# A hybrid attention and recurrence block: both value projections as one block product of seven, attention weights by differences of the values, and gate inputs kept in DRAM

## The chip, the cores and the metric

The kernel runs on one core of a Trainium2 chip. The core has a matrix engine (TensorE, PE in the profile), three engines for elementwise work (VectorE or DVE, ScalarE or ACT, GpSimd or POOL), a fifth engine that only issues transfers (SyncE or SP), and 16 DMA engines that move data between DRAM and the two on-chip memories, SBUF (operands, 128 partitions) and PSUM (results of matmuls, 8 banks of 512 columns of fp32). The metric is the device time of one execution in microseconds, lower is better; a kernel's time is the median of several executions.

## The reference

One layer on x (1024 tokens x 1024 channels, fp32), followed by a final RMSNorm:

```python
xn = rmsnorm(x, norm1_g);  u = xn @ w_in           # 3*512 + 4*512 + 2*1024 columns
q_sb, k_sb, v_sb, f_raw, i_hg, q_hg, g_hg, gate_sb, gate_hg = split(u)
# stick-breaking attention, 8 heads of 64; for query t and key s < t:
A[t, s] = sigmoid(z_ts) * prod_{s<j<t} (1 - sigmoid(z_tj)),   z = q.k / 8
o_sb = A @ v_sb
# gated recurrence (HGRN2), 4 heads of 128: S_t = diag(f_t) S_{t-1} + (1 - f_t) i_t^T, o_t = S_t^T q_t
o_hg = rmsnorm(hgrn2(silu(q_hg), f, i_hg)) * silu(g_hg)
merged = sigmoid(gate_sb + b) * (o_sb @ w_o_sb) + sigmoid(gate_hg + b) * (o_hg @ w_o_hg)
h = x + merged @ w_out
h = h + square(relu(rmsnorm(h, norm2_g) @ w_ff1)) @ w_ff2
return rmsnorm(h, final_g)
```

v_sb (512 columns) and i_hg (512 columns) are the values of the attention and of the recurrence; both are plain projections of xn.

## The kernel before, in words

Operands of matmuls are split in two: a high part, rounded by a cast (ScalarE, `hi_copy`, line 144), and a low part, the remainder (VectorE, `lo_sub`, line 149). A product is then three matmuls, high x high, high x low and low x high (`three`, line 526). One helper issues all matmuls (line 121), another all transposes (line 124), another SP's loads (line 129), so in the profile they share a line and are told apart by their tiles: pjqk, pjf, pjq, pjg are projections, pjv and pji the two value projections, z the attention's scores, pw the transposed weights, po its output, pga and pgq parts of the gate projections, gX and gY the gate products.

The program is written straight out, with no loop on the chip. A scheduler assigns each engine its instructions in order, from the order in which they are written, their data and a few hand-made order edges (`after`). TensorE's work is written in two lanes: "main" (attention, recurrence) and "fill" (projections that nobody waits for at once). Fill work is cut into steps of a few matmuls and dealt out between the pieces of the main lane: a stream `st` holds a list of jobs (one job: split its weights, then the steps of its matmuls, then an epilogue), `st.advance(n, upto)` issues n steps, `st.finish(upto)` the rest of the jobs up to a number. While one job runs, the next job's weights are split and those of the one after are loaded (`prefetch`); the first job has nobody ahead of it to do so. `turns` holds the order of ScalarE's and VectorE's instructions during the first norms as written.

The stages, with rough times in the profile:

- 0 to 50 us: x is loaded, normalised, transposed and split into `xn` (high and low, by token half and pairs of k-tiles). Beside that, head 0's q and k, and the values of heads 0 to 3 ("quad 0", `first_job`, `token_steps`): per block of 128 tokens 8 k-tiles x 3 matmuls of 256 columns. The first block runs its matmuls on the weights' high parts first (`lo_last`).
- 50 to 315 us: the attention, 64 items (8 heads x 8 query blocks, in the order 7, 0, 6, 1, 5, 2, 4, 3). For an item `scores` makes z and two sigmoids from it, bt = sigmoid(z) and rm = sigmoid(-z); `weights` runs a product scan over rm from the right on VectorE (line 777) and multiplies bt by it (line 157); `turn` transposes bt on TensorE and splits it into high and low; `values` multiplies by V. In between come 126 fill steps: q and k of heads 1 to 7, the values' quad 1, the recurrence's f, q, first values (`i_job`, 256 columns wide again) and g of head 0.
- 302 to 580 us: the recurrence, head by head (`hg_levels`, then `hg_tail` beside the next head's levels), with fill steps at the rates `FILL`: the other recurrence projections, `raw_job` (eight, each a block of the gate projections that needs no sums) and `sb_job` (the attention's output projection).
- 500 to 600 us: `whole_input` adds xn's high and low parts back together by DMA, and `sum_forms` makes sums and differences of its four blocks and splits them: forms 6, 5, 7 and 3, for the gate projections, which are already a 2x2 by 2x2 block product of seven (`GatePair`: x6, y5, x7, y3).
- 580 us to the end: gates, output projection and the MLP.

Of the kernel before, what the change touches and what calls it, by code (L numbers as in the profile page):

```python
# [39 lines left out]
def kernel(  # L40
# [37 lines left out]
    def slot_n(name, n, dt=F32):  # L78

        if n <= 512:  # L80
            return hpool.tile([P, 512], dt, tag="h", name=name)
        return slot(name, dt)

# [440 lines left out]
    st = Stream()  # L524
# [109 lines left out]
    vt, qk, osb = {}, {}, {}  # L634

    def v_epilogue(quad):


        def ep(ps, tb):
            if tb % 2 == 0:  # L640
                vt[quad, tb // 2] = slot(f"V{quad}_{tb // 2}", F32R)
            V = vt[quad, tb // 2].rearrange("p (t h s d) -> p t h s d", t=2, h=4, s=2)
            src = ps.rearrange("p (h d) -> p h d", h=4)
            hi_lo(V[:, tb % 2, :, 0, :], V[:, tb % 2, :, 1, :], src)

        return ep

    def v_stat(h, tb):
        c = ((tb % 2) * 4 + h % 4) * P
        return vt[h // 4, tb // 2][:, c : c + P]  # L650
# [15 lines left out]

    def v_unit(quad):
        return wide_unit(f"wv{quad}", W_IN, C_V + quad * 256)

    def v_job(quad):  # L670
        unit = v_unit(quad)
        return st.add(
            [unit], lambda: token_steps(f"pjv{quad}", unit, xn, range(NT), v_epilogue(quad))
        )
# [27 lines left out]

    def first_job():
        name, u_qk, ep = qk_item(0)
        u_qk.__class__ = FirstUnit
        u_v = v_unit(0)

        def body():
            v_ep = v_epilogue(0)
            for half, parts in enumerate((((0, 2), (2, 2)), ((0, 4),))):  # L710
                ps = bank(f"{name}_{half}")
                for b0, n in parts:
                    ts = slice(b0 * P, (b0 + n) * P)
                    yield from proj_half(ps[:, ts], u_qk.hl[0], xn.mov, KT, half, ts=ts)
                    if b0 + n == 4:
                        ep(ps, half)
                    if half == 0 and b0 > 0:
                        st.prefetch()
                    tb = 4 * half + b0
                    yield from token_steps("pjv0", u_v, xn, range(tb, tb + n), v_ep, tb == 0)  # L720

        return st.add([u_qk], body), u_qk, u_v

    j_first, u_qk0, u_v0 = first_job()
    j_qk = {0: j_first}
    for h in range(1, NHS):
        j_qk[h] = proj_jobs([qk_item(h)], xn)
        if h == 4:
            v_job(1)
# [6 lines left out]
    def scores(h, qb):  # L736
# [3 lines left out]
        bt, rm = slot_n(f"bt{h}_{qb}", nk), slot_n(f"rm{h}_{qb}", nk)  # L740
        step = 320 if nk == 640 else 512
        for s0 in range(0, nk, step):
# [3 lines left out]
            for i, Q in enumerate((QH, QL)):  # L746
# [7 lines left out]
            c0, e = int(s0 == 0), m - (s0 + m == nk)  # L754
            nc.scalar.activation(  # L755
                rm[:, s0 + c0 - 1 : s0 + m - 1], z[:, c0:m], AF.Sigmoid, scale=-0.125
            )
            nc.scalar.activation(bt[:, s0 : s0 + e], z[:, :e], AF.Sigmoid, scale=0.125)  # L758
        lastsel[0] = nc.gpsimd.memset(bt[:, nk - 1 : nk], 0.0)
        zs[h, qb] = (bt, rm)  # L760
# [4 lines left out]
    nc.vector.tensor_copy(bits[:, 1024 - P - 1 : 1023], ident)  # L765

    def weights(h, qb):
# [4 lines left out]
        bt, rm = zs[h, qb]  # L772
        cut = qb == NT - 1
        parts = ((512, nk - 1), (0, 512)) if cut else ((0, nk - 1),)
        for i, (a, b) in enumerate(parts):
# [11 lines left out]
            m = mul(bt[:, a:b], bt[:, a:b], rm[:, a:b])  # L787
            if qb == 5:
                after(m, turn_lo[0])

    def turn(h, qb, between):

        open_block("main")
        bt, rm = zs.pop((h, qb))
# [14 lines left out]
        if par == 0:  # L809
            for t in tiles[-1]:  # L810
                after(nc.gpsimd.memset(t[:, (nkb - 1) % 4, qs].bitcast(F32), 0.0), lastsel[0])
        order = list(enumerate(tiles))
        for i, (th, tl) in order[::-1] if qb == NT - 1 else order:
# [10 lines left out]
            turn_lo[0] = hi_lo(  # L824
                th[:, 0:n, qs], tl[:, 0:n, qs], pw[:, : n * P].rearrange("p (k q) -> p k q", q=P)
# [60 lines left out]
    def i_job(h):  # L886
        unit = wide_unit(f"wi{h}", W_IN, C_I + h * P)

        def ep(ps, tb):
            for j in range(2):  # L890
                if tb == 0:
                    hg[h + j, "v"] = slot(f"v{h + j}")
                nc.scalar.copy(hg[h + j, "v"][:, tb * P : (tb + 1) * P], ps[:, j * P : (j + 1) * P])

        unit.late = h == 0

        def body():
            for i, _ in enumerate(token_steps(f"pji{h}", unit, xn, range(NT), ep)):
                yield
                if unit.late and i == 6:  # L900
                    hi_behind[0] = turn_hi[0]
                    st.prefetch()
                    hi_behind[0] = None

        return st.add([unit], body)
# [10 lines left out]

    def hg_jobs(h):
        for key, c0, ep in (
            ("f", C_F, f_epilogue(h)),
            ("q", C_QH, silu_epilogue(h, "q")),  # L920
            ("g", C_GH, silu_epilogue(h, "g")),
        ):
            if key == "g" and h % 2 == 0:
                i_job(h)
            u = cols_unit(f"w{key}{h}", [(W_IN, c0 + h * P, P)])
            j_hg[h] = proj_jobs([(f"pj{key}{h}", u, ep)], xn)

    hg_jobs(0)
# [224 lines left out]
    class Split:  # L1153
# [18 lines left out]
    scratch = ctx.enter_context(  # L1172
        tc.tile_pool(name="scratch", bufs=1, space=bass.MemoryType.DRAM)
    )

    def dram(name, shape):
        return scratch.tile(shape, F32, tag=name, name=name)

    def half(name, dt=F32):
        return hpool.tile([P, 512], dt, tag="h", name=name)  # L1180

# [74 lines left out]
    def raw_job(cb):  # L1256
# [13 lines left out]
        def body():  # L1270
# [13 lines left out]
            if cb == 3 or cb == KT - 1:  # L1284
                whole_input(1, int(cb == KT - 1))
# [15 lines left out]
    forms, whole = {}, {}  # L1301
    WAIT = 5

    def whole_input(i, j):
        for kp in range(2):
            h, l = (t.bitcast(F32) for t in xn.t[i, 2 * j + kp])
            nc.gpsimd.dma_start(l, h, accum_op=ALU.add)
            whole[i, j, kp] = l

    def sum_forms():  # L1310


        raw = whole
        def split(m, kp, src):
            forms[m, kp] = tuple(slot(f"gs{n}{m}{kp}", F32R) for n in "hl")
            hi_lo(*forms[m, kp], src)

        for j in range(2):
            whole_input(0, j)
        yield from range(WAIT)  # L1320
        s1, s2 = {}, {}
        for kp in range(2):
            s1[kp], s2[kp] = slot(f"gs1{kp}"), slot(f"gs2{kp}")
            ins = add(s1[kp], raw[1, 0, kp], raw[1, 1, kp])
            if kp == 0:
                after(ins, hg_sum[0])
            yield
            sub(s2[kp], s1[kp], raw[0, 0, kp])
            yield
            split(6, kp, s2[kp])  # L1330
            yield
        for kp in range(2):
# [785 lines left out]
    for tb in range(3, NT):  # L2118
        load_x(tb)
# [181 lines left out]
```

## Time and profile before

| | |
|---|---|
| time, median of 3 runs | 1449.7 us (1448.64 to 1451.11) |
| the profiled execution's own time | 1450.06 us |
| its span, first to last instruction | 1448.3 us |
| busy: TensorE, VectorE, ScalarE, GpSimd | 1433.5, 1101.4, 668.4, 146.7 us |
| moved by DMA | 225.73 MB, mean 156 GB/s |
| granted TensorE clock | 0.999 |

How to read it: a profile's times count from the first instruction. A group of instructions is given by line, engine, operation and tiles (out<-in); then their number, busy time and mean duration, the engine's idle time just before them, and what ended it. Matmuls overlap in the record, each lasting longer than the time until the next begins, so for TensorE the time from start to start counts, not the duration. A window gives for each engine its busy time and, in brackets, its number of instructions, in the order PE, PEld (weight loads), DVE, ACT, POOL, as far as they have any; then the granted clock, the DMA engines' share and GB/s.

### The profile page before, as it was taken

What the parts mean: (1) busy time and instruction counts of PE and PEld (TensorE: products, weight loads), DVE (VectorE), ACT (ScalarE), POOL (GpSimd) and SP (SyncE); (2) the same over time, 40 slices, a digit from 0 to 9 for tenths busy, and PEclk for the clock granted to TensorE, in tenths of its full rate; (3) what the DMA queues carried; (4) which work ended last, traced back from release to release, by engine and by line L of the source; (5) the groups of instructions that cost most, each with busy time, mean ns of one, the idle gap of its engine ahead of it and who ended that gap; (6) DMA issues with size and microseconds to landing.
All of it is one profiled execution on the core that took longest, in us unless ns stands there. A gap on an engine that the chain in (4) does not pass through costs nothing. (4 is left out here: it accounts for less than half of the span.)

```text
span 1448.3 us, 19992 instructions
## 1 busy us (share of the span) xinstructions
PE 1433.5 (99%) x7470; PEld 1220.8 (84%) x7470; DVE 1101.4 (76%) x1571; ACT 668.4 (46%) x1156; POOL 146.7 (10%) x344
## 2 busy tenths in 40 slices
PE   9999999999999999999999999999999999999997
PEld 8989988988898888888887888888888888888886
DVE  6699899798747797887776898666666757768765
ACT  7566666652323243523243675444444533523343
POOL 3121121110000012100010300000000000000042
PEclk9999999999999999999999999999999999999999
DMA  7234154321303349655469514344445974776724
GB/s 212 48 99 102 37 95 81 60 44 52 103 16 102 73 138 258 233 166 177 146 188 312 192 59 164 134 153 160 151 155 193 344 275 175 256 271 251 277 101 180
DMA packets 157913, 225.73 MB, mean 156 GB/s; under 512 B 25676, under 2 KB 93816, under 8 KB 157816
## 3 DMA queue, kind: packets, MB, share of 16 engines
q1 hardware_dynamic: 141976, 181.19, 37.3%
q0 software_dynamic: 12096, 36.71, 10.3%
q10 hardware_dynamic: 3744, 6.56, 1.2%
q8 instruction: 59, 0.97, 0.3%
q14 instruction: 38, 0.31, 0.1%
HBM read 162.55 MB, written 61.87 MB: 155 GB/s over the span
## 5 line engine op out<-in xcount | busy, mean ns | idle before, releaser
L144 ACT CAST whid<-w 128x1024 fp32r<-128x1024 f32 x30 | 31.6, 1053 | 153.4 <-PE pm L121 85.5
L777 DVE TENSOR_TENSOR_SCAN rm<-rm,bits 128x511 f32<-128x511 f32 (+7 forms) x72 | 87.3, 1220 | 14.2 <-ACT rm L755 12.7
L121 PE MATMUL pm<-wlod,sh 128*128 128x512 f32 x240 | 93.5, 389 | 0.0
L121 PE MATMUL pm<-whid,sh 128*128 128x512 f32 x240 | 93.4, 389 | 0.0
L121 PE MATMUL pm<-whid,sl 128*128 128x512 f32 x240 | 93.4, 389 | 0.0
L121 PE MATMUL pm<-tl,sh 128*128 128x512 f32 (+1 forms) x210 | 81.3, 387 | 0.0
L121 PE MATMUL pm<-th,sl 128*128 128x512 f32 (+1 forms) x210 | 81.3, 387 | 0.0
L121 PE MATMUL pm<-th,sh 128*128 128x512 f32 (+1 forms) x210 | 81.3, 387 | 0.0
L149 DVE TENSOR_TENSOR wlod<-w,whid 128x1024 fp32r<-128x1024 f32 x30 | 36.7, 1224 | 56.0 <-ACT whid L144 56.0
L149 DVE TENSOR_TENSOR sl<-sa,sh 128x1024 fp32r<-128x1024 f32 x56 | 68.3, 1220 | 0.5 <-ACT sh L144 0.5
L144 ACT CAST wTh<-pw 128x128 fp32r<-128x128 f32 (+3 forms) x96 | 44.4, 487 | 50.2 <-PE pw L124 42.6
L1950 POOL TENSOR_SCALAR fss<-fss 128x1 f32<-128x1 f32 x8 | 4.4, 547 | 562.4 <-ACT fsc L1945 561.9
L144 ACT CAST sh<-sa 128x1024 fp32r<-128x1024 f32 x56 | 57.2, 1046 | 7.3 <-DMA sa<-ad 7.3
L149 DVE TENSOR_TENSOR wTl<-pw,wTh 128x512 fp32r<-128x512 f32 (+3 forms) x96 | 50.7, 547 | 8.8 <-ACT wTh L144 6.3
L121 PEld LDWEIGHTS pm<-wlod,sh 128*128 128x128 f32 x240 | 45.0, 188 | 9.8 <-DVE wlod L149 0.4
L121 PEld LDWEIGHTS pm<-whid,sl 128*128 128x128 f32 x240 | 45.1, 188 | 9.4
L121 PEld LDWEIGHTS pm<-whid,sh 128*128 128x128 f32 x240 | 45.1, 188 | 9.2
L157 DVE TENSOR_TENSOR bt<-bt,rm 128x511 f32<-128x511 f32 (+7 forms) x72 | 49.0, 686 | 4.9 <-ACT bt L758 1.0
L121 PE MATMUL pX<-sql,t1h 128*128 128x512 f32 x128 | 50.0, 391 | 0.4 <-DVE sql L149 0.4
L121 PE MATMUL pX<-sqh,t1h 128*128 128x512 f32 x128 | 50.0, 390 | 0.0
L121 PE MATMUL pX<-sqh,t1l 128*128 128x512 f32 x128 | 49.8, 389 | 0.0
L755 ACT ACTIVATE rm<-z 128x511 f32<-128x511 f32 (+6 forms) x96 | 47.5, 501 | 4.6 <-DVE bt L157 1.9
(924 smaller groups left out, 4598.7 us busy)
## 6 DMA issues: line engine op xcount, KB each, us to landing
w<-in_w_ff_dram SPq DMA_DIRECT2D x72, 512.0 KB, 5.9
sa<-ad SPq DMA_DIRECT2D x56, 512.0 KB, 6.9
ad<-a SPq DMA_DIRECT2D x32, 256.0 KB, 4.2
ad<-s SPq DMA_DIRECT2D x16, 512.0 KB, 5.5
tw<-in_w_out_dram POOLq DMA_DIRECT2D x24, 256.0 KB, 4.1
x<-in_x_dram SPq DMA_DIRECT2D x8, 512.0 KB, 8.7
xnl<-xnh POOLq DMA_DIRECT2D x8, 512.0 KB, 10.8
pr<-pd SPq DMA_DIRECT2D x8, 512.0 KB, 6.5
```

The source lines that it names most:

```text
L121: return pe(nc.tensor.matmul(*a, **k))
L144: hi_last[0] = after(in_turn("act", nc.scalar.copy(dst, src)), hi_behind[0])
L149: nc.vector.tensor_tensor(out=dst, in0=src, in1=hi.bitcast(F32), op=ALU.subtract),
L157: return nc.vector.tensor_tensor(out=out, in0=a, in1=b, op=ALU.mult)
L755: nc.scalar.activation(rm[:, s0 + c0 - 1 : s0 + m - 1], z[:, c0:m], AF.Sigmoid, scale=-0.125)
L777: sc = nc.vector.tensor_tensor_scan(out=rr, data0=rr, data1=bits[:, 1024 - nk + a : 1024 - nk + b][:, ::-1], initial=rm[:, b : b + 1] if i ...
L1950: nc.gpsimd.tensor_scalar(out=ssq, in0=ssq, scalar1=1.0 / D, scalar2=EPS, op0=ALU.mult, op1=ALU.add)
```

## The change

The two value projections become one product: xn as 2x2 blocks (token halves by halves of the 1024 channels) times the weights as 2x2 blocks (channel halves by attention's and recurrence's 512 columns), with seven block products in place of eight. Each is 4 token blocks x 4 k-tiles x 3 matmuls of 512 columns. It stands ahead of the attention; products 1 and 2, on plain blocks of the first token half, stand among the first norms in place of quad 0. Products 3, 5, 6 and 7 need sums and differences of xn's blocks: xn is added together on VectorE (`early_whole`), summed (`early_op`), split (`early_form`), and the split forms are stored to DRAM, where the gates read them back later instead of making them (`whole_input` and the old `sum_forms` go). The results are stored to DRAM by rows (`vrows`, `irows`) and loaded back by head.

The attention's weights are taken apart: with R_s the product of rm from s on, the weight is R_{s+1} - R_s, so that A @ v is the sum over s of (R_s - 1)(v_{s-1} - v_s). bt, its sigmoid and its product go; the scan runs over nk instead of nk - 1 columns; rm is transposed; 1 is subtracted as it is split (a bias on ScalarE, a scalar on VectorE); the values of a head are loaded twice, one row apart, subtracted and split (`v_load`, `v_split`).

The order of the fill jobs changes: head 1's q and k are finished ahead of the products (it is now the first job of `st`), raw jobs 0 and 1 move into the attention, g of recurrence head 0 out of it; 86 fill steps are left there. `FILL` is changed, and x6 and y5 of the first gate pair move into the last recurrence tail.

The diff, cut to its core:

```diff
+    class ValuePair:
+        WEIGHT = {1: "11", 2: "21", 3: "22", 4: "21", 5: "11", 6: "22", 7: "12"}
+        def sums(self):
+            for kp in range(2):
+                b11, b12, b21, b22 = (self.raw[b, kp] for b in ("11", "12", "21", "22"))
+                sub_(b11, b12, b11)
+                sub_(b12, b22, b12)
+                sub_(b22, b22, b11)
+                sub_(b21, b21, b22)
+        def steps(self, m, banks, start):
+            for k in range(4):
+                wh, wl = (t[:, (k % 2) * 512 : (k % 2 + 1) * 512] for t in self.hl[m, k // 2])
+                for tb, ps in banks.items():
+                    three(ps, *self.stat(m, k, tb), wh, wl, start and k == 0, k == 3, True)
...
+        def x7(self):
+            self.product(7, self.X, False)
+            for tb in range(4):
+                self.u3[tb] = half(f"vu3{tb}")
+                nc.scalar.copy(self.u3[tb], self.X[tb])
+                v = self.p4[tb]
+                nc.vector.tensor_tensor(out=v, in0=v, in1=self.X[tb], op=ALU.add)
+                self.store(vrows, 1, 1, tb, v)
...
+    def early_form(m, *src):
+        for kp, r in enumerate(src):
+            vi.form[m, kp] = tuple(slot(f"ef{n}{m}{kp}", F32R) for n in "hl")
+            hi_lo(*vi.form[m, kp], r)
+            for i, t in enumerate(vi.form[m, kp]):
+                nc.gpsimd.dma_start(formd[m, kp][:, i, :], t.bitcast(F32))
...
     def scores(h, qb):
-            nc.scalar.activation(
-                rm[:, s0 + c0 - 1 : s0 + m - 1], z[:, c0:m], AF.Sigmoid, scale=-0.125
-            )
-            nc.scalar.activation(bt[:, s0 : s0 + e], z[:, :e], AF.Sigmoid, scale=0.125)
-        lastsel[0] = nc.gpsimd.memset(bt[:, nk - 1 : nk], 0.0)
+            nc.scalar.activation(rm[:, s0 : s0 + m], z[:, :m], AF.Sigmoid, scale=-0.125)
     def weights(h, qb):
-            m = mul(bt[:, a:b], bt[:, a:b], rm[:, a:b])
     def turn(h, qb, between):
-                transpose(pw[:, kb * P : (kb + 1) * P], bt[:, s0 : s0 + P])
-            turn_lo[0] = hi_lo(th[:, 0:n, qs], tl[:, 0:n, qs], pw...)
+                transpose(pw[:, kb * P : (kb + 1) * P], rm[:, s0 : s0 + P])
+                    nc.scalar.activation(th[:, 0:n, qs], src, AF.Identity, bias=minus_one),
+                nc.vector.scalar_tensor_tensor(
+                    out=tl[:, 0:n, qs], in0=src, scalar=-1.0,
+                    in1=th[:, 0:n, qs].bitcast(F32), op0=ALU.add, op1=ALU.subtract,
...
     def sum_forms():
+        yield from range(7)
+        for i, m in enumerate((6, 5, 7, 3)):
+            for kp in range(2):
+                forms[m, kp] = tuple(slot(f"gs{n}{m}{kp}", F32R) for n in "hl")
+                for j, t in enumerate(forms[m, kp]):
+                    load(t.bitcast(F32), formd[m, kp][:, j, :])
+                yield
...
-    u_v0.roomy = (1,)
-    u_v0.load(1)
+    vi.load("11", 0)
     load_x(2)
-    u_v0.load()
-    for tb in range(3, NT):
+    vi.load("11", 1)
+    load_x(3)
+    vi.load("21", 0)
+    load_x(4)
+    vi.load("21", 1)
+    for tb in range(5, NT):
...
-    st.advance(4, 1)
-    u_v0.split()
+    front.advance(4, 1)
+    vi.split(1)
     norm1((2, 3))
-    st.advance(3, 1)
+    front.advance(4, 1)
     norm_transpose(xn, 0, 2, 2)
-    st.advance(5, 1)
+    vi.split(2)
     norm1(range(4, NT))
-    st.advance(4, 1)
+    front.advance(12, 1)
     norm_transpose(xn, 1, 0, 4)
     turns["on"] = False
+    for kp in range(2):
+        for b in ("12", "22"):
+            vi.load(b, kp)
+    st.jobs[0][0][0].load()
...
+    front.advance(4, 1)
+    vi.sums()
+    front.finish(j_first)
+    for half_, j in ((1, 0), (1, 1), (0, 0)):
+        early_whole(half_, j)
+    early_op((1, 1), (1, 0), (1, 1), ALU.add)
+    st.finish(j_qk[1])
+    vi.split(4)
+    vi.x4()
+    early_op((1, 0), (0, 0), (1, 0), ALU.subtract)
+    early_op((0, 0), (1, 1), (0, 0), ALU.subtract)
+    early_form(6, *early_at((0, 0)))
+    vi.split(6)
+    vi.x6()
+    early_form(7, *early_at((1, 0)))
+    early_whole(0, 1)
+    early_op((0, 1), (0, 1), (0, 0), ALU.subtract)
+    vi.split(7)
+    vi.x7()
+    early_form(5, *early_at((1, 1)))
+    vi.split(5)
+    v_load(0)
+    for kp in range(2):
+        vi.load("22", kp)
+    vi.y5()
+    early_form(3, *early_at((0, 1)))
+    vi.split(3)
     scores(*items[0])
     weights(*items[0])
+    v_split(0)
     scores(*items[1])
+    st.jobs[1][0][0].split()
+    vi.y3()
-    n_fill = 9 * (j_hg[0] - j_qk[0]) + 18
+    n_fill = 9 * 6 + 2 * 7 + 2 * 9
...
+        ahead = it[0] + 1
+        if ahead < NHS and i % NHS in (2, 5):
+            (v_load if i % NHS == 2 else v_split)(ahead)
...
-    FILL = (3.75, 3.3, 2.8, 2.6, 3)
+    FILL = (4.5, 3.0, 2.6, 2.65, 3.6)
+                    if h == NHG:
+                        tails += 1
+                        if tails == 4:
+                            st.finish(j_sb[3])
+                            gp[0].x6()
+                        elif tails == 5:
+                            gp[0].y5()
```

More of the change, by code (lines that the diff above doesn't have):

```diff
@@ L82, in slot_n, with dram, half @@
         return slot(name, dt)
+    scratch = ctx.enter_context(
+        tc.tile_pool(name="scratch", bufs=1, space=bass.MemoryType.DRAM)
+    )
+    def dram(name, shape):
+        return scratch.tile(shape, F32, tag=name, name=name)
+    def half(name, dt=F32):
+        return hpool.tile([P, 512], dt, tag="h", name=name)
     def bank(name):
@@ L665, in qk_epilogue @@
         return ep
[L667 to L673, printed above, removed]
-        )
     def qk_item(h):
@@ L703, in first_job @@
+    irows = dram("irows", [T, HGW])
+    vi = ValuePair()
     def first_job():
@@ L715, in body @@
                     if b0 + n == 4:
[L716 to L726, printed above, removed]
-        j_qk[h] = proj_jobs([qk_item(h)], xn)
-        if h == 4:
-            v_job(1)
+                        ep(ps, half_)
@@ L884, in f_epilogue, with i_load @@
         return ep
[L886 to L905, printed above, removed]
+    def i_load(h):
+        hg[h, "v"] = slot(f"v{h}")
+        nc.gpsimd.dma_start(
+            chunks(hg[h, "v"]),
+            irows[:, h * P : (h + 1) * P].rearrange("(t p) c -> p t c", p=P),
+        )
     def silu_epilogue(h, key):
@@ L1171 @@
     mgs = Acts("ms")
[L1172 to L1180, printed above, removed]
     def add(out, a, b):
```

291 lines of the change are left out of this document (192 added, 99 removed).

## The prediction

> **What bounds the kernel now.** I read the page first, then who waited for whom on TensorE, then the chain that ended last, then timelines of the start, then windows by stage.
>
> ```profile
> span 1448.3 us, 19992 instructions
> PE 1433.5 (99%) x7470; PEld 1220.8 (84%) x7470; DVE 1101.4 (76%) x1571; ACT 668.4 (46%) x1156; POOL 146.7 (10%) x344
> PEclk9999999999999999999999999999999999999999
> ```
> ```profile
> PE warm L121 <- POOL ident masks.py:199: 2.2, 1, 2.2
> PE pwX L121 <- DVE h L1186: 2.0, 1, 2.0
> PE hnt L124 <- DVE hn L1571: 1.6, 1, 1.6
> ```
> ```profile
> 855.46 8.16 PE pX L121 x36
> 1135.94 299.53 PE pm L121 x1320
> ```
>
> The reader is to see a TensorE that hardly ever waits, at the full clock: the three longest waits of the run make 5.8 us together. A busy share alone would prove little, since matmuls overlap in the record. The two rows of the chain prove it: 36 matmuls of 512 columns in 8.16 us and 1320 in 299.53 us are both 0.227 us from start to start, so the rhythm is the same in quite different stages. The time is therefore TensorE's work plus the idle time that someone adds. Whatever is taken off VectorE, ScalarE or GpSimd alone is worth nothing here.
>
> The 256-column matmuls have a rhythm of their own; these rows are the first and the last of 20 in a row, then two rows 20 matmuls apart among those of 512 columns:
>
> ```profile
> 401.73 0.28 PE L121 MATMUL pji<-wi2l,xnh 128*128 128x256 f32 x1
> ...
> 404.01 0.28 PE L121 MATMUL pji<-wi2h,xnl 128*128 128x256 f32 x1
> ```
> ```profile
> 34.76 0.39 PE L121 MATMUL pjqk<-xnh,wqk0whi 128*128 128x512 f32 x1
> ...
> 39.30 0.39 PE L121 MATMUL pjqk<-xnh,wqk0wlo 128*128 128x512 f32 x1
> ```
>
> 19 steps in 2.28 us are 0.120 us; 20 steps in 4.54 us are again 0.227 us. So 256 columns cost a little over half of 512.
>
> **The work on TensorE.** The two value projections are removed whole; asked for by tile (attention's, then the recurrence's):
>
> ```profile
> 0.00:1449.00 1449.00, 48.55 (x384) 47.41 (x384) 6.38 (x16) 5.88 (x16) 1.00 0.49 156
> ```
> ```profile
> 0.00:1449.00 1449.00, 48.65 (x384) 47.19 (x384) 6.90 (x32) 1.00 0.49 156
> ```
>
> Removed: 768 matmuls of 256 columns x 0.120 = 92.2 us. Added: seven products of 4 token blocks x 4 k-tiles x 3 = 48 matmuls of 512 columns, 336 x 0.227 = 76.3 us. Net 15.9 us less. Scores, transposes (of rm in place of bt), the values' products and everything after are as many as before; x6 and y5 of the first gate pair only move. That is the whole gain on the path.
>
> The Trainium skill, "TensorE: Matmul & The Clock Gate", section Back-to-back issue gap, gives for one isolated stream at full clock N / 2.4 + 2.5 ns: 109 ns for 256 columns, 216 for 512. By that rule the trade would be an estimated 83.8 against 72.5 us, 11.3 us gained, and the result 4.6 us later than mine. The trace differs (120 and 227 ns, with three-matmul groups of changing weights), and the trace decides; the rule gets no chance.
>
> **The attention stage.**
>
> ```profile
> 50.00:302.00 252.00, 251.88 (x1611) 227.05 (x1611) 221.91 (x316) 165.76 (x383) 49.40 (x181) 1.00 0.35 74
> ```
> ```profile
> L777 DVE TENSOR_TENSOR_SCAN rm<-rm,bits 128x511 f32<-128x511 f32 (+7 forms) x71 | 86.1, 1220 | 14.2 <-ACT rm L755 12.7 <-POOL bt L759 1.3
> L149 DVE TENSOR_TENSOR wTl<-pw,wTh 128x512 fp32r<-128x512 f32 (+3 forms) x90 | 47.5, 547 | 8.8 <-ACT wTh L144 6.3 <-PE pw L124 2.0
> L157 DVE TENSOR_TENSOR bt<-bt,rm 128x511 f32<-128x511 f32 (+7 forms) x70 | 47.5, 684 | 4.8 <-ACT bt L758 1.0 <-issue 0.2
> ```
>
> The stage (windows by engine: PE, PEld, DVE, ACT, POOL) loses VectorE's product with bt, 47.5 us, and ScalarE's second sigmoid. But its fill work shrinks too: the second value quad (192 x 0.120 = 23.0), the recurrence's first values (23.0), one g projection and qk of head 1 (48 x 0.227 = 10.9 each) leave; two raw gate jobs (36 matmuls, 8.2 each) come in. TensorE: 252 - 67.8 + 16.4 = about 201 us. VectorE: 221.9 - 47.5, less some 15 of lows and epilogues that go with those projections (at 1.2 a weight, 0.4 a value block, 0.7 a half bank), plus seven value splits of two half-width operations at about 0.7 and the raw jobs' 9: about 178 us. That is 89% against 88% before, and at 88% TensorE stood fully packed. So cover and load fall together: I cost it at nothing, from 0 to 4 us (2% of the stage). The loads of the values from DRAM are asked for three items ahead, 3 x 201 / 64 = 9.4 us; 512 KB of weights in the same 256-byte pieces land in about 4 us:
>
> ```profile
> DMA to landing us min/median/max: 4.1/4.3/4.4
> ```
>
> (the two halves of head 1's q and k weights). Uncovered they would cost that much once per head. The new Identity with a bias sits between sigmoids; a table load at each change would be 1.28 us:
>
> ```profile
> L755 ACT ACT_TABLE_LOAD x1 | 1.3, 1283 | 1.6 <-PE z L121 1.6
> ```
>
> ```profile
> 743.28 0.72 ACT L1456 ACTIVATE gu<-gu,prm 128x512 f32<-128x512 f32 x1 [4.13 <-DVE gu L1183]
> 746.01 0.59 ACT L1646 ACTIVATE h<-pwW 128x512 f32<-128x512 f32 x1
> ```
>
> But the second pair of rows is a sigmoid (the gate) and the Identity that follows it, with no load between them. Nothing.
>
> **Ahead of the attention**, where VectorE and ScalarE must now feed seven products, I find the new waits. Timelines of VectorE, ScalarE and TensorE at the start:
>
> ```profile
> 9.85 3.23 DVE L325 SCALAR_TENSOR_TENSOR xnl<-xnt,prm,xnh 128x256 fp32r<-128x256 f32 x8
> 13.34 2.36 DVE L149 TENSOR_TENSOR wv0l<-wv0r,wv0h 128x1024 fp32r<-128x1024 f32 x2 [0.27 <-ACT wv0h L144]
> 22.71 0.41 DVE L149 TENSOR_TENSOR V<-pjv,V 128x256 fp32r<-128x256 f32 x1
> 28.50 0.75 DVE L630 TENSOR_SCALAR x<-x,n_y 128x1024 f32<-128x1024 f32 x1 [0.43 <-POOL n_y L243]
> 29.29 0.69 DVE L149 TENSOR_TENSOR KS<-pjqk,KS 64x512 fp32r<-64x512 f32 x1
> 30.61 1.21 DVE L149 TENSOR_TENSOR wqk1l<-wqk1r,wqk1h 128x1024 fp32r<-128x1024 f32 x1
> 32.40 5.34 DVE L325 SCALAR_TENSOR_TENSOR xnl<-xnt,prm,xnh 128x512 fp32r<-128x512 f32 x8
> ```
> ```profile
> 12.21 2.04 ACT L144 CAST wv0h<-wv0r 128x1024 fp32r<-128x1024 f32 x2
> 19.06 3.03 ACT L322 ACTIVATE xnh<-xnt,prm 128x256 fp32r<-128x256 f32 x8 [2.15 <-PE xnt L124]
> 26.54 0.58 ACT L144 CAST KS<-pjqk 64x512 fp32r<-64x512 f32 x1
> ```
> ```profile
> 13.47 0.28 PE L121 MATMUL pjv<-wv0h,xnh 128*128 128x256 f32 x1
> 18.70 1.85 PE L124 MATMUL xnt<-ident,x 128*128 128x128 f32 x13 [0.16 <-DVE x L630]
> 30.19 3.66 PE L124 MATMUL xnt<-ident,x 128*128 128x128 f32 x32
> ```
>
> A, the first product. The old first value block ran all its matmuls on high weights first (lo_last). The new p1 needs the low part in its second matmul, at 13.47 + 0.23; the first low is done at 13.34 + 1.18 = 14.5. Wait: 0.8 us.
>
> B, the second product. After p1 of two blocks (24 x 0.227 = 5.4) TensorE is at 19.7; 16 transposes at 0.114 end at 21.5. p2 follows, and its weights are split behind the normalised second pair of blocks, since ScalarE and VectorE are held in written order there: casts until 19.7 + 0.4 + 3.0 = 23.1, high part 24.1, low part 25.3, against 21.7. Wait: 3.6 us. If the transposes go ahead of p1's second block, that block covers it and 0.6 is left. I take 3.6: in the trace, too, the transposes began only once the first blocks' matmuls were issued.
>
> C, q and k of head 1. Its job is the first of its stream, so nobody prefetches it, and its low part is ordered behind QL of head 0's second half. That QL is done some 0.2 + 0.58 + 0.69 + 0.69 = 2.1 us behind its bank's last matmul, head 1's low part 1.2 later, 3.3; the first matmul that needs it is due 0.45 after that last one. So at least 2.9 us, with TensorE's fill lane shut behind it. More, if VectorE is late. TensorE, from B: p2 of two blocks until 31, the second half of head 0's first bank (24 x 0.120) until 34, p1 of two blocks until 39.3, 32 transposes until 43, p2 of two blocks and the second half of head 0's q and k (2 x 5.4) until 54. VectorE has the low parts of x done at 39.7 + 5.3 = 45 and 9.7 us until KS at 54.8. In them belong two additions of p2 (1.4), four sums of x (at 1.21, the 1024-wide operation: 4.9) and two of the first form (2.4): 8.7 us. The eight sums of the weights (9.8 us) and two more sums of x (2.4) must fit in before. There VectorE is free from 26.5 to 39.7, less four scalings (3.0), two additions and KS and QL (1.4 each): 7.4 us. What is left over, 4.8, less the 1.0 to spare, goes on top: 3.8. Wait: about 6.5 us, from 2.9 up to 14 if none of the 12.2 fitted in before (12.2 - 1.0 + 2.9).
>
> D, the rest. The last column of this window, the start, is the rate at which transfers run when many are asked for:
>
> ```profile
> 0.00:13.50 13.50, 11.16 (x72) 10.68 (x73) 7.68 (x19) 8.12 (x17) 3.64 (x13) 1.00 0.94 293
> ```
>
> Between products VectorE has four low parts of weights and forms (4.9 us) and some sums (2.4 to 4.9) in TensorE's 10.9 us; a bank is read in 0.7 us, while the next product starts on another. The forms' 16 loads in the recurrence's tail, 8.4 MB, need 29 us at 293 GB/s, and 29 fill steps of 6 matmuls (39 us) cover them; the gates' and weights' loads on SP's queue stand behind them. On GpSimd's queue 16 stores of forms and 16 of values go ahead of head 1's row copies at most, which scores need four products later. The recurrence's values are loaded when a head begins and used in its tail, a head later. x6 and y5 of the first gate pair stood between the last head's split (1.02 + 1.21 us) and its product; x7, 12 x 0.227 = 2.7 us, still does. Nothing, then; from 0 to 5 us if a handover or a load comes late.
>
> Sum: -15.9 + 0.8 + 3.6 + 6.5 = -5.0 us. The profiled execution took 1450.06 us (span 1448.3 and 1.8 around it), 0.4 over the median; so 1445.1 for it, and 1444.7 as a median.
>
> **Rivals.** First, the covers work: only the waits that no order avoids remain, 0.8 + 0.6 + 2.9 = 4.3, and 1438. For it speaks that TensorE's waits of today are so few; against it that C's order is written out.
>
> Second, slower: VectorE's sums in C lie bare. The four further weight blocks (2 MB, 7 us at 293 GB/s) need free slots; if they get them only when the last x blocks are transposed, at about 43 us, they land at 50, the sums all come late, and C is 14 us: -15.9 + 0.8 + 3.6 + 14 + 2 for the first handover behind it = +4.5, so 1454. It decides from a landing of about 45 us on. Against it: x0 to x3 free four slots at 22 us.
>
> Third, the cover in the attention is too thin or the form loads hold up the tail: another 4 us, 1449, which is no change. TensorE's time per item falls from 252 / 64 = 3.9 to 3.1 us while the scan's mean stays at 1.2.
>
> Fourth, the named parts do nothing by themselves: the bt product and sigmoid are off the path. That is in my sum already.
>
> **How the numbers follow.** Chances: my sum 0.43, covers work 0.26, third 0.18, slower 0.13. A measurement of this kernel tells about 0.2%, 2.9 us, from no change. Faster than 1446.8: the first two, 0.69. Within: 0.18. Slower: 0.13. The range leaves out a tenth at each end: 1436, a little under the covers' case (the bounds of D and the attention allow no gain), to 1453, just short of the slow case.
>
> **What would show it.** TensorE's matmuls should be 48 x 7 of 0.227 us and none of the 768; its waits should name the low part of the first product's weights (about 1 us), of the second's (3 to 4) and wqk1's (3 to 8), all ahead of the first scan; from 60 to 270 us it should stay packed. Wrong would be: VectorE as releaser many times within the attention; TensorE waiting for a form's or a weight's DMA; waits of over 14 us ahead of the attention; or none at all.

## The result and the profile after

The changed kernel takes 1481.5 us (median of 4 runs, 1480.26 to 1486.32) against 1449.4 us before (4 runs, 1448.64 to 1451.11): ratio 1.0226, 95% interval 1.0201 to 1.0251. It is 32 us slower, where 5.0 us faster was forecast. Its profiled execution took 1482.33 us, span 1480.5.

The page of the changed kernel, its first lines and the row of the granted clock:

```profile
span 1480.5 us, 18978 instructions
PE 1433.2 (97%) x7038; PEld 1195.8 (81%) x7038; DVE 1096.8 (74%) x1536; ACT 648.1 (44%) x1042; POOL 173.5 (12%) x330
PEclk9899999999999999999999999999999999999999
```

TensorE has 7038 instructions, 432 fewer than before, which is just 768 removed and 336 added. So the trade was made as described; yet the span is longer, and the clock row has dips that it had not. Who waited for whom on TensorE (total us, times, longest):

```profile
PE pjqk L131 <- DVE wqk1l L159: 11.0, 1, 11.0
PE po L131 <- DVE wTl L1000: 6.3, 2, 5.9
PE z L131 <- DVE wTl L1000: 2.9, 1, 2.9
...
PE pjqk L131 <- ACT wqk1h L154: 2.2, 1, 2.2
PE viX L131 <- DVE viwlo L159: 1.8, 1, 1.8
PE viZ L131 <- ACT vih L154: 1.7, 1, 1.7
PE viP L131 <- DVE QL L159: 1.7, 1, 1.7
```

Before, no wait was over 2.2 us. Now one of 11.0 us stands ahead of the attention, and two, 5.9 and 2.9 us, within it, all for VectorE, which is busy no longer in all than before (1096.8 against 1101.4 us). A busy share would never have shown this.

To put one number on each stretch I take, for every matmul and transpose, the time until the next one starts, less the median of that time among its own kind (same tiles, same columns) in the same kernel. The sum is TensorE's lost time; idle time and half clock both count:

| us lost by TensorE | 0 to 125 us | 125 to 400 us | from 400 us | together |
|---|---|---|---|---|
| before | 1.0 | 2.7 | 8.2 | 11.9 |
| changed | 30.8 | 19.6 | 7.7 | 58.1 |

Span less lost time is TensorE's work: 1448.3 - 11.9 = 1436.4 before, 1480.5 - 58.1 = 1422.4 now. So 14.0 us of work went, and 46.2 us of lost time came: +32.2, the difference of the spans. What has to be explained is 29.8 us at the start and 16.9 in the attention.

**The start.** SyncE's issues, and in a page row their median time to landing (last column):

```profile
23.98 6.12 SPq L139 DMA_DIRECT2D vi<-in_w_in_dram  x4
30.16 1.16 SPq L139 DMA_DIRECT2D wqk1r<-in_w_in_dram  x2
```
```profile
vi<-in_w_in_dram SPq DMA_DIRECT2D x10, 512.0 KB, 4.3
```

The four further weight blocks were asked for by 30.1 us, and by the median landed at about 34.4; head 1's weights were asked for by 31.3. VectorE's timeline from there:

```profile
39.94 0.68 DVE L159 TENSOR_TENSOR QL<-pjqk,QH 64x512 fp32r<-64x512 f32 x1
44.70 5.36 DVE L335 SCALAR_TENSOR_TENSOR xnl<-xnt,prm,xnh 128x512 fp32r<-128x512 f32 x8 [4.08 <-ACT xnh L332]
...
52.46 1.22 DVE L738 TENSOR_TENSOR vi<-vi,vi 128x1024 f32<-128x1024 f32 x1
...
54.73 6.89 DVE L738 TENSOR_TENSOR vi<-vi,vi 128x1024 f32<-128x1024 f32 x6
...
62.14 1.22 DVE L738 TENSOR_TENSOR vi<-vi,vi 128x1024 f32<-128x1024 f32 x1
...
64.69 5.75 DVE L878 TENSOR_TENSOR xw<-xnh,xnl 128x1024 f32<-128x1024 f32 x5
70.36 2.34 DVE L889 TENSOR_TENSOR xw<-xw,xw 128x1024 f32<-128x1024 f32 x2
72.63 1.21 DVE L159 TENSOR_TENSOR wqk1l<-wqk1r,wqk1h 128x1024 fp32r<-128x1024 f32 x1
```

The reader is to see the order. VectorE stands idle for 4.08 us at 40.6 although the weights of the sums (L738) have been there for some 6 us; the first sum comes at 52.46, behind the low parts of x's second half. Then eight sums of weights, six of x (L878) and two of a form (L889) run ahead of wqk1l, for which TensorE waits. The sums of the weights fill the room until 63.4, ahead of KS and QL; so seven of the eight other sums come behind QL, 64.7 to 72.7, where nothing covers them. Its rows, and two windows (PE, PEld, DVE, ACT, POOL, clock, DMA share, GB/s):

```profile
62.52 0.40 PE L131 MATMUL pjqk<-xnl,wqk1h 128*128 128x512 f32 x1
73.89 0.79 PE L131 MATMUL pjqk<-xnh,wqk1l 128*128 128x512 f32 x1 [10.97 <-DVE wqk1l L159]
74.48 0.63 PE L131 MATMUL pjqk<-xnh,wqk1h 128*128 128x512 f32 x1
74.91 0.63 PE L131 MATMUL pjqk<-xnl,wqk1h 128*128 128x512 f32 x1
...
77.02 0.39 PE L131 MATMUL pjqk<-xnh,wqk1h 128*128 128x512 f32 x1
77.25 0.40 PE L131 MATMUL pjqk<-xnl,wqk1h 128*128 128x512 f32 x1
```
```profile
25.00:50.00 25.00, 23.08 (x110) 18.43 (x111) 13.66 (x21) 12.86 (x22) 6.60 (x12) 0.86 0.47 138
50.00:75.00 25.00, 11.82 (x49) 9.12 (x49) 24.36 (x32) 3.27 (x5) 2.20 (x4) 0.77 0.10 31
```

From 50 to 75 us VectorE is full (24.36 of 25) and TensorE half empty, while in the 25 us before VectorE was busy only 13.66. Behind the wait TensorE goes from 74.48 to 74.91 in 0.43 us, and 2 us later in 0.23: half clock for a while.

**The attention.** SyncE asks for the two halves of the second gate block (the row spans both issues, the second at 262.5); their time to landing; VectorE:

```profile
237.16 25.71 SPq L139 DMA_DIRECT2D wga1r<-in_w_in_dram  x2
```
```profile
DMA to landing us min/median/max: 9.6/9.6/9.6
```
```profile
266.86 0.27 DVE L1000 SCALAR_TENSOR_TENSOR wTl<-pw,wTh 128x128 fp32r<-128x128 f32 x1
272.26 1.23 DVE L1339 TENSOR_TENSOR wga1r<-wga1r,wga1r 128x1024 f32<-128x1024 f32 x1 [5.13 <-DMA wga1r<-in_w_in_dram]
273.41 1.75 DVE L946 TENSOR_TENSOR_SCAN rm<-rm,bits 128x768 f32<-128x768 f32 x1
```

A raw job needs both of the two weight buffers at once. The second half can be asked for only when the weights ahead of it, head 7's q and k, have been split (VectorE's wqk7l, 261.20 to 262.43), 25 us after the first half. VectorE's next instruction in order then waits for it, with the scan and the low parts of the attention's weights behind it. Block 0 does the same at 184.31, after a wait of 4.66 us.

The second half is not only asked for late, it is also slow. At the same moment GpSimd asks for the next head's values, which the new attention reads back from DRAM:

```profile
262.47 2.52 POOL L657 DMA_DIRECT2D vr<-vrows  x2
```

These two loads land in 8.6 and 8.5 us, and the DMA engines are busy 0.90 of the 10 us from 262 on. With block 0 it is the same: values asked for at 174.90, its second half at 175.63. How much of the wait comes from this company, and how much from asking late, was not tried apart.

### The profile page after: what moved, and what is told of

Its sections match the earlier page's. It is cut to its first block, busy times and chain, and to the rows that moved or that the text cites. A ratio compares the mean times of both kernels' runs of the same rounds, so it can differ in the third digit from the quotient of the medians.

```text
span 1480.5 us, 18978 instructions
## 1 busy us (share of the span) xinstructions
PE 1433.2 (97%) x7038; PEld 1195.8 (81%) x7038; DVE 1096.8 (74%) x1536; ACT 648.1 (44%) x1042; POOL 173.5 (12%) x330
## 4 chain that ended last, share of the span: by engine, by line
PE 85%; DVE 7%; DMA 3%; ACT 2%; issue 2%; POOL 0%; SPq 0%; DVEq 0%; ACTq 0%; POOLq 0%
PE pm L131 20%; PE pX L131 9%; PE pY L131 6%; PE pW L131 5%; PE pjqk L131 5%; PE pys L131 3%; PE pjq L131 3%; PE gX L131 3%; PE gY L131 3%; PE pyh L131 3%; PE po L131 3%; PE pjf L131 2%; PE sl L131 2%; PE pjg L131 2%; PE pga L131 2%; PE z L131 2%
## 5 line engine op out<-in xcount | busy, mean ns | idle before, releaser
L946 DVE TENSOR_TENSOR_SCAN rm<-rm,bits 128x512 f32<-128x512 f32 (+6 forms) x72 | 87.1, 1219 | 6.4 <-ACT rm L920 5.4
L994 ACT ACTIVATE wTh<-pw,minus_one 128x512 fp32r<-128x512 f32 (+2 forms) x96 | 53.2, 581 | 44.2 <-PE pw L134 42.5
L1000 DVE SCALAR_TENSOR_TENSOR wTl<-pw,wTh 128x512 fp32r<-128x512 f32 (+2 forms) x96 | 50.2, 545 | 15.0 <-ACT wTh L994 13.7
L131 PE MATMUL po<-wTl,V 128*128 128x256 f32 x160 | 41.5, 293 | 6.4 <-DVE wTl L1000 6.3
L131 PEld LDWEIGHTS pm<-th,sh 128*128 128x128 f32 x210 | 39.5, 188 | 8.1
```

The costliest lines, as they stand in the source:

```text
L131: return pe(nc.tensor.matmul(*a, **k))
L946: sc = nc.vector.tensor_tensor_scan(out=rr, data0=rr, data1=bits[:, 1024 - nk + a : 1024 - nk + b][:, ::-1], initial=rm[:, b : b + 1] if i ...
L994: nc.scalar.activation(th[:, 0:n, qs], src, AF.Identity, bias=minus_one),
L1000: nc.vector.scalar_tensor_tensor(out=tl[:, 0:n, qs], in0=src, scalar=-1.0, in1=th[:, 0:n, qs].bitcast(F32), op0=ALU.add, op1=ALU.subtract,),
```

## The experiments

Theory one had two separate causes: at the start the order of VectorE's work (wqk1l behind the sums), in the attention the late second half of the raw jobs' weights. Its rivals: a thinner cover that lets VectorE's work lie bare whatever its order, and the attention by parts itself. All of these kernels compute the whole reference. The kernel before stood beside each batch and took 1450.0, 1450.6 and 1449.2 us.

**Head 1's weights split ahead of the sums.**

```diff
     first_row()
+    st.jobs[0][0][0].split()
     front.advance(4, 1)
     vi.sums()
```

> The changed kernel with one line more: the weights of head 1's q and k are split ahead of the sums of the value weights instead of behind the sums of x. Theory one (VectorE's written order ahead of the attention holds the fill lane): TensorE's waits of 11.0 and 2.2 us on wqk1l and wqk1h go, and with them the half-clock stretch behind them (13.65 us at half speed in the changed kernel); the sums that stood before are then covered by the 10.9 us of head 1's q and k, so 1481.5 falls by 10 to 15 us to about 1466 to 1471. Rival one (VectorE's backlog only moves on: x4 waits for its weights' low part instead): less than 4 us, 1478 or more, with a new wait of 8 us or more on viwlo. Either way it stays slower than before's 1449.

Measured 1471.3 us (ratio to before 1.0145, 1.0129 to 1.016): 10.3 us back. TensorE's waits for head 1's weights:

```profile
PE pjqk L131 <- ACT wqk1h L154: 1.6, 1, 1.6
...
PE pjqk L131 <- DVE wqk1l L159: 0.5, 1, 0.5
```

The 11.0 is 0.5. The eight sums of the weights are all still there; only one instruction changed its place. Lost at the start: 19.5 us; in the attention 19.1, as before this edit, so the two causes are separate.

**Raw jobs 0 and 1 behind the attention** (with g of head 0 back in).

```diff
-    j_raw = [raw_job(0)]
+    j_raw = []
     for h in range(5, NHS):
         qk_job(h)
-    j_raw.append(raw_job(1))
     hg_job(0, "f")
     hg_job(0, "q")
-    j_first_hg = j_hg[0]
     hg_job(0, "g")
+    j_first_hg = j_hg[0]
     hg_jobs(1)
-    j_raw.append(raw_job(2))
+    j_raw += [raw_job(cb) for cb in range(3)]
...
-    n_fill = 9 * 6 + 2 * 7 + 2 * 9
+    n_fill = 9 * 6 + 3 * 9
```

> The changed kernel with raw jobs 0 and 1 back behind the recurrence's head 1 projections, and g of recurrence head 0 in the attention in their place (81 fill steps instead of 86). Theory one (VectorE stands in order behind the late second weight block of each raw job, 4.7 and 5.1 us, and TensorE behind the transposed weights' low parts): the waits of 2.9 and 6.3 us on wTl go, and the two half-clock stretches in the attention (3.4 and 6.8 us) with them; 1481.5 falls by 10 to 15 us to about 1467 to 1472. Rival two (attention by parts itself, its cover or its chain, makes the waits): at most 3 us, 1478 or more, and the waits on wTl stay.

Measured 1470.2 us (1.0136, 1.0119 to 1.0153): 11.4 back. The waits in the attention now:

```profile
PE po L131 <- DVE wTl L1000: 2.4, 6, 0.6
```

No wait for VectorE is over 0.6 us. Lost there: 7.5 us in place of 19.6, although the fill is five steps thinner. What is left, 4.8 above before, I put down to the thinner cover, which no run takes alone; the rest was the raw jobs in this place.

**The block product with the attention's old form** (bt, two sigmoids, the values read back once).

```diff
-            nc.scalar.activation(rm[:, s0 : s0 + m], z[:, :m], AF.Sigmoid, scale=-0.125)
+            nc.scalar.activation(
+                rm[:, s0 + c0 - 1 : s0 + m - 1], z[:, c0:m], AF.Sigmoid, scale=-0.125
+            )
+            nc.scalar.activation(bt[:, s0 : s0 + e], z[:, :e], AF.Sigmoid, scale=0.125)
...
+            m = mul(bt[:, a:b], bt[:, a:b], rm[:, a:b])
```

> The changed kernel with the attention's weights as before (two sigmoids, the product bt times rm, transposes of bt); the values are loaded once per head and split without a difference. Theory one: the front and the raw jobs are as in the changed kernel, and VectorE's work in the attention rises by about 47 us to some 225 us where TensorE has about 201 us of work, so the stage becomes VectorE's: 15 to 40 us slower than the changed kernel, 1497 to 1522. Rival two (attention by parts is what slows the attention): as fast as the changed kernel or faster, 1482 or less.

Measured 1490.7 us (1.0275, 1.0258 to 1.0292), 9.2 over the changed kernel. Less than I had expected (15 at least), but the rival, that the new attention is what slows it, falls: TensorE loses 26.5 us in the attention in place of 19.6, 12.1 of it, in place of 6.3, in the waits of this row:

```profile
PE po L131 <- DVE wTl L159: 12.1, 12, 3.0
```

**The attention by parts with the old projections** (the old value projections write their rows to DRAM, and the new attention reads them).

```diff
-            hi_lo(V[:, tb % 2, :, 0, :], V[:, tb % 2, :, 1, :], src)
+            v = half(f"vo{quad}_{tb}")[:, 0:256]
+            nc.scalar.copy(v, ps)
+            nc.gpsimd.dma_start(
+                vrows[1 + tb * P : 1 + (tb + 1) * P, quad * 256 : (quad + 1) * 256], v
+            )
```

> The kernel before with attention by parts alone: both value projections, the order of the jobs and the gate inputs as before; only the attention's values go by way of DRAM, are loaded twice one row apart, subtracted and split. TensorE's work is the same as before. Theory one (nothing on VectorE or ScalarE is on the path as long as TensorE is covered): 1449 within 4 us, no stall on wTl over 1 us. Rival two (attention by parts slows by its chain: transposed weights' high part with a bias at 581 ns in place of 487, loads of values in 256-byte rows): slower by 8 us or more. That the removed 47 us of VectorE and 48 us of ScalarE are worth something: faster by more than 3 us.

Measured 1451.9 us (1.0013, 1.0004 to 1.0023): worth nothing alone, if anything 2 us slower. The window of the attention, before and in this kernel:

```profile
125.00:400.00 275.00, 274.66 (x1743) 245.32 (x1742) 236.50 (x388) 144.62 (x329) 37.83 (x132) 1.00 0.31 69
125.00:400.00 275.00, 274.19 (x1737) 244.75 (x1736) 208.59 (x337) 129.86 (x268) 48.43 (x102) 1.00 0.35 80
```

VectorE has 208.59 us there in place of 236.50 before, and TensorE was full in both. Under a full TensorE, 28 us off VectorE buy nothing.

**Both moves together.** The first two edits in one kernel.

> The changed kernel with both earlier moves: head 1's query/key weights are split ahead of the weight sums, and the first two gate jobs stand behind the attention. Theory one (two separate causes, the low part at the start and the late gate weights in the attention, each with its own idle time of TensorE): the gains add, 10.3 + 11.4 us from 1481.5, so 1457 to 1462 us. Rival (the two share a cause, VectorE's backlog, so that the time won at the start is lost again in the attention): 1465 to 1470 us.

Measured 1456.7 us (1.0042, 1.0027 to 1.0057): 24.8 below the changed kernel, a little more than 10.3 + 11.4 and just under the range. The gains add, the rival falls.

**Raw jobs left in the attention, with a buffer more.**

```diff
             super().__init__(f"wga{cb}", dmas)
+            if cb < 2:
+                self.roomy = (1,)
```

> Head 1's weights split early as before, the first two gate jobs left in the attention, but the second half of their weights in a slot of its own, so that its load need not wait for the second of the two weight buffers. Theory one (the cost in the attention is VectorE standing behind a load that was asked for late): nearly all of the 11.4 us that moving these jobs out gave comes back, 1459 to 1463 us. Rival (the gate jobs cost that time by their own operations, sums and splits on VectorE, wherever their weights lie): within 3 us of the kernel with the early split alone, 1468 to 1472 us.

Measured 1460.0 us (1.0064, 1.0047 to 1.0081), beside 1471.3 with the early split alone: 11.3 us back with the raw jobs where they were. SyncE now asks for the two halves of the first block within 9 us. Its row, and the first sum of the two in this kernel and in the one with the early split alone:

```profile
140.08 8.95 SPq L139 DMA_DIRECT2D wga0r<-in_w_in_dram  x2
```
```profile
L1339 DVE TENSOR_TENSOR wga0r<-wga0r,wga0r x1: 1193/1193/1193, 167.3 to 167.3; 128x1024 f32<-128x1024 f32 x1
L1339 DVE TENSOR_TENSOR wga0r<-wga0r,wga0r x1: 1226/1226/1226, 171.7 to 171.7; 128x1024 f32<-128x1024 f32 x1
```

With the early split alone VectorE waited 4.2 us for the second half of the first block and 6.0 us for that of the second; here it waits for neither. So the cost was the load that landed late, not the jobs' sums and splits on VectorE, which are all still there.

**The opening reordered too**, over both moves.

```diff
     front.advance(4, 1)
+    vi.split(2)
     norm_transpose(xn, 0, 2, 2)
-    vi.split(2)
+    st.jobs[0][0][0].load()
+    for kp in range(2):
+        for b in ("12", "22"):
+            vi.load(b, kp)
     norm1(range(4, NT))
     front.advance(12, 1)
+    st.jobs[0][0][0].split()
+    vi.sums((0,))
     norm_transpose(xn, 1, 0, 4)
...
     vi.split(6)
+    early_form(7, *early_at((1, 0)))
     vi.x6()
-    early_form(7, *early_at((1, 0)))
+    vi.split(7)
     early_whole(0, 1)
     early_op((0, 1), (0, 1), (0, 0), ALU.subtract)
-    vi.split(7)
     vi.x7()
```

> Both moves, and the rest of the opening in another order: the second product's weights are split ahead of the second pair of token blocks, head 1's weights and the last weight blocks are loaded ahead of the last norms, half of the weight sums stands ahead of the second half's transposed blocks, and the seventh product's input forms are split ahead of the sixth product. Theory one (the waits at the start are all questions of VectorE's and ScalarE's order, the engines have room): the waits of 1.8, 1.9, 1.0, 1.2, 2.0 and 1.1 us that are left go, with two spells of half clock of some 1.4 us each, so about 11 us below both moves together, 1446 to 1452 us. Rival (VectorE has no room ahead of the attention, an earlier split only moves the wait to the next operand): at most 3 us below both moves together, 1456 to 1460 us.

Measured 1446.8 us (0.9978, 0.9967 to 0.9989), 0.2% faster than before. The moves were made at once; what each of them is worth was not tried. Lost at the start: 11.5 us in place of 19.5. Two waits are new or left:

```profile
PE xnt L134 <- DVE xnl L335: 3.8, 2, 3.3
...
PE viP L131 <- DVE QL L159: 1.8, 1, 1.8
```

The sums now stand partly ahead of the low parts of x's second half, which hold a bank that a transpose needs: the wait has a new place, and the granted clock was at half for 3.4 us from 42.6.

**That opening refined.**

```diff
-    vi.sums((1,))
+    vi.sums((1,), turns["dve"])
...
+    early_op((1, 0), (0, 0), (1, 0), ALU.subtract)
     st.finish(j_qk[1])
-    vi.split(4, (1,))
     vi.x4()
-    early_op((1, 0), (0, 0), (1, 0), ALU.subtract)
```

(x4 splits its second half of weights two steps in; `early_op` is ordered behind the last QL written.)

> The reordered opening with its two longest waits that are left taken on: the second half of the weight sums may start only behind the last low part of the normalised input (the fourth transposed bank waited 3.5 us for it, and half a clock of some 1.4 us followed), and the last early sum and the fourth product's second split stand behind head 1's q and k (a bank waited 1.9 us for them). Theory one (VectorE's order is the cause, its work fits): about 6 us below the reordered opening's 1446.8, 1439 to 1443 us. Rival (VectorE's time from 50 to 75 us is full, 24.87 of 25 us, so that sums put off come to lie ahead of the sixth product's forms): 1445 to 1449 us.

Measured 1445.0 us (1444.61 to 1445.22; 0.9964, 0.9952 to 0.9977), 4.2 us or 0.3% below before and 36.5 below the changed kernel. It gained 1.8 over the one before it, not 6, and the kernel before itself differs by 1.4 between the two batches. The transposed bank's wait fell to 1.1, but QL's stayed:

```profile
PE viP L131 <- DVE QL L159: 1.6, 1, 1.6
PE xnt L134 <- DVE xnl L335: 1.6, 2, 1.1
```

That result lies between the two ranges I had given, on the rival's (1445 to 1449) edge; VectorE is still busy 24.88 of the 25 us from 50 to 75, so its room there is used up.

**The same opening with the old attention.**

The kernel just told, with the old attention's edit from above.

> The same opening and the gate jobs behind the attention, but the attention in its form of before (two sigmoids, scan, multiply; the values read back once). It tells how much of the gain needs the attention by parts. If the 9.2 us that the old form cost inside the changed kernel are its VectorE and ScalarE work under a thin cover, they show here too: 4 to 10 us above the other kernel of this pair. If they were mostly its collision with the late gate weights, less than 3 us above it.

Measured 1462.0 us (1459.7 to 1463.18; 1.0081, 1.0068 to 1.0095): 17.1 above its pair, more than either case. The profiled execution is the fastest, 1459.7. The attention's window with the refined opening and the new attention, then with the old one, and TensorE's longest waits with the old one:

```profile
125.00:400.00 275.00, 272.54 (x1589) 234.64 (x1588) 239.99 (x375) 153.36 (x300) 62.57 (x142) 1.00 0.45 103
```
```profile
125.00:400.00 275.00, 259.36 (x1496) 219.62 (x1495) 262.08 (x413) 169.42 (x380) 56.32 (x189) 0.99 0.38 83
```
```profile
PE po L131 <- DVE wTl L159: 10.2, 12, 2.2
PE pw L134 <- DVE bt L167: 3.9, 5, 1.9
```

With the old form VectorE is busy 262.08 of 275 us and TensorE loses 25.7 us; with the new one 239.99, and 7.1 lost. In the changed kernel the same step cost only 9.2, with the raw jobs' waits there and five steps more of fill; how much of the difference is due to which was not tried. The lost time of all runs, and the two parts against each other:

| kernel | time, us | lost 0 to 125 | 125 to 400 | from 400 |
|---|---|---|---|---|
| changed | 1481.5 | 30.8 | 19.6 | 7.7 |
| head 1's weights split early | 1471.3 | 19.5 | 19.1 | 8.8 |
| raw jobs out | 1470.2 | 33.5 | 7.5 | 6.5 |
| both moves | 1456.7 | 19.5 | 7.5 | 7.1 |
| early split, raw jobs with own buffer | 1460.0 | 19.4 | 8.2 | 7.9 |
| opening reordered | 1446.8 | 11.5 | 6.8 | 5.5 |
| opening refined | 1445.0 | 8.5 | 7.1 | 5.9 |
| product, old attention | 1490.7 | 31.8 | 26.5 | 9.3 |
| refined opening, old attention | 1462.0 | 5.5 | 25.7 | 5.5 |
| parts, old projections | 1451.9 | 1.9 | 3.2 | 9.4 |

| us | old attention | attention by parts |
|---|---|---|
| old projections | 1449.4 | 1451.9 |
| block product, refined opening, raw jobs out | 1462.0 | 1445.0 |

Neither part is worth anything alone in the forms tried; only together, and in a good order, do they gain, and then 0.3%. (The product alone was tried only in the orders made for both.)

## Why the prediction was wrong

**TensorE's work, -15.9 us: right.** The count is exact, the median spacing of the added products is 0.227 us, and span less lost time fell by 14.0; for the refined opening, 1443.0 - 21.4 = 1421.6, it fell by 14.8. The trade stands at about its forecast.

**A, 0.8 us: right in kind.** TensorE waited 0.4 us for the first product's low part.

**B, 3.6 us: right in mechanism.** 1.7 us for the second product's high part and 0.5 for its low part; half clock behind it, which I had not priced, took some 13 matmuls at 0.43 in place of 0.23, 2.6 us more. The cure was the one implied: with the split written ahead of the second pair of blocks both waits are gone.

**C, 6.5 us: the first step that failed.** Waits of 2.2 and 11.0 us and about 1.5 of half clock, 14.7 us: the worst end of my range. (The sum's own parts, 2.9 and 3.8, make 6.7.) I filled VectorE's idle time ahead of 45 us with the sums, as if an engine took whatever is ready. VectorE took its instructions in the order that was compiled, idle for 4.08 us beside landed operands, and that order put all eight sums behind the low parts of x's second half. My slower rival had the price, 14 us, but the wrong condition: it was to decide by the weights' landing, from 45 us on. They landed at about 34, and the sums came late all the same. Moving one split gave 10.3 us back, and the whole order of the opening another 9.9 (1456.7 to 1446.8).

**The attention, nothing (0 to 4): the second step that failed.** It cost 16.9 us. I compared load with cover, 89% with 88%, and there I was not far off: with the raw jobs out, or with a buffer more, 4.8 to 5.5 us above before remain, close to the third rival's 4. The other 11 to 12 us came from a thing that the sum of loads does not hold: I had counted the raw jobs' matmuls and VectorE's work, and not that one needs both weight buffers, nor who stands behind a VectorE that waits for it. The values' loads, put at about 4 us, took 3.8 to 8.8, with a median of 6.3; TensorE waited for none of them. I had named VectorE as a releaser within the attention as the sign that would prove me wrong; so it did.

**D, nothing (0 to 5): in its range.** 1.8 for the seventh product's weights, 0.9 for its forms and 1.7 for a bank, 4.4 us. Two small waits at either end of the start I had not listed: 1.6 us for the first low parts of x ahead of head 0's q and k, and 0.7 for the attention's first sigmoid. All these make 26.6 of the 29.8 us at the start; the rest I did not take apart.

**The fourth rival** said that bt and its sigmoid are off the path. With the old projections that is shown (1451.9). With the block product it is not: there they are worth 9 to 17 us. The likely reason is that the product takes 46 us of fill out of the attention, so that VectorE's time, 262.08 of 275 us with the old form, comes to lie bare. My sum needed this part of the change and gave it no price.

**The rule of the Trainium skill that I weighed** ("TensorE: Matmul & The Clock Gate", section Back-to-back issue gap), 109 and 216 ns a matmul, would have made the trade an estimated 11.3 us. The measured fall of work, 14.0 to 14.8, is nearer to the traced 15.9.

**The whole:** -14.0 + 29.8 at the start + 16.9 in the attention - 0.5 behind it = +32.2 us.

## What to carry to other kernels

When matmuls are traded for sums on another engine, write down that engine's order around the trade, instruction by instruction: idle time ahead of an instruction that stands behind a late one can't be used, and one split in the wrong place cost 10 us here. Of a job that moves, count the buffers that it must hold at once, and name what stands behind the engine that will wait for them. A part that is worth nothing alone under a full TensorE can be the part that makes another one pay, so try the parts in all combinations.

## What the runs showed of the hardware

After waits the granted clock was at half for 6.83 us from 25.8, 13.65 us from 63.3, 3.41 us from 186.2 and 6.83 us from 274.9 in the changed kernel, in multiples of 3.41; 512 columns then took 0.43 us from start to start. It made up some 5.8 of the 46 us (30 matmuls). The Trainium skill, "TensorE: Matmul & The Clock Gate", section What's actually happening, gives 3413 ns for the window by which the clock is set, which these lengths agree with, and an idle window of that length as the cause. The early split shows half clock with less: waits of 1.6 and 0.5 us, and then

```profile
60.00:65.00 5.00, 4.00 (x10) 2.89 (x11) 4.96 (x7) 1.95 (x3) 1.10 (x2) 0.66 0.15 39
```

a granted clock of 0.66 over these 5 us. With the opening refined, where no wait was over 1.6 us once the first matmuls had run, the granted clock reads 1.00 in each 25 us of the first 125.

The second half of the second gate block, 512 KB, asked for at 262.5, took 9.6 us to land, within 0.1 us of the two value loads; with a buffer of its own it was asked for at 229.3, also in the attention but 10 us behind a pair of value loads, and landed in 3.7 us.
